# Layer 1's mixer weights split once, kept in DRAM scratch, and fetched in two parts

## The chip, the cores and the metric

The kernel runs on one core of a Trainium2 chip. The metric is device time in microseconds (us) for one execution; three runs of the kernel before took 1915.36, 1915.76 and 1921.28 us, median 1915.76. TensorE is called PE, VectorE DVE, ScalarE ACT, GpSimd POOL; SP issues most of the DMAs, POOL the others. PE's clock stands at one of two levels, 1.2 or 2.4 GHz; the profile gives it as a share of the higher one.

## The reference, cut to what matters

Two layers; the latent stream has 512 tokens, the context stream 256, both 1024 wide. Both use the same weights. In layer 1 the context serves only for its keys and values.

```python
for i in range(DEPTH):                       # DEPTH = 2
    last = i == DEPTH - 1
    # adaln: six modulation vectors of 1024 from ada_w[i] (1024 x 6144)
    h_l = rmsnorm(x, norm1_g[i]) * (1.0 + sc1_l) + sh1_l
    h_c = rmsnorm(ctx, norm1_g[i]) * (1.0 + sc1_c) + sh1_c
    p_l = h_l @ w_in[i]                      # hyena | gated MLP | attention
    p_c = h_c @ w_in[i]
    # queries of x attend to the keys of ctx and of x in one softmax
    x = x + g1_l * mix_out(p_l, att_l, hy_params, sg_params, w_out[i])
    x = x + g2_l * swiglu(rmsnorm(x, norm2_g[i]) * (1.0 + sc2_l) + sh2_l, ffn_w1[i], ffn_w2[i])
    if not last:
        ...                                  # the same for ctx
```

Inside `mix_out`, hyena convolves with filters computed by a small network from the weights alone (`hyena_filters`), through a Fourier transform that the kernel does with tables.

## The kernel before, in words

**Products in three parts.** Each float32 operand is split into a high part (rounded by an ACT copy) and a low part (a DVE subtraction), in `split` (L230 to L233). `mm3` (L251 to L253) then makes three matmuls, each on 128x128 blocks.

**Weights.** `weights` (L235) loads a weight tile of at most 128x1024 (512 KB) through SP into the arena FW and splits it into two blocks of the arena RW. RW holds 24 units of 256 floats per partition, that is three split tiles; FW holds six raw ones. `Columns` makes two such tiles out of `w_out` or the feed-forward weights, `win` two out of a chunk of `w_in`, `proj_cm` uses one. In layer 1 the context and the latent stream each load and split the chunks 7 to 10 of `w_in` for themselves.

**Arenas.** R (104 units) holds activations and tables. A task that will need room there first reserves it with `claim` and gives it back with `unclaim`; while the sum of reservations would pass 104, `claim` yields "wait" and the task goes no further. F (44 units) holds float32 data.

**Order.** The program is written by tasks in `network`: `lat_task`, `con_task`, `side_task` (the hyena filters' spectra, `spectra`), `ada_task` (the modulation vectors). `woven` takes the next step of the task that has least cost for its rate; a step that says "wait" costs a little and writes nothing. So a task that cannot get its reservation stands still while others go on writing. A scheduler then fixes one order for each engine, which the engine follows without overtaking; each instruction waits for semaphores of what it reads or overwrites.

**The end of layer 0's mixer.** `second` of `lat_mixer` ends the projections; the word "late" is set, and `spectra` of layer 1 may then start: it reserves 18*2+4 = 40 units. The latent stream meanwhile runs `outproj` over six of eight groups (24 units) and the second attention (`attend`, 12 units, with the latent queries, keys and values' 24 and the context keys and values' 8), and reserves 32 units for the input of its feed-forward part. The context's own feed-forward input holds 16. `ada_task` writes layer 1's six sections at the same time: 48 loads of 512 KB into FW, each pair followed by eight small matmuls (L400), with no wait but FW. Layer 0's feed-forward part (`ffn`, both streams) follows, then layer 1.

Of the kernel before, what the change touches and what calls it, by code (L numbers as in the profile page):

```python
# [16 lines left out]
P = 128  # L17
# [21 lines left out]
class Buf:  # L39


    def __init__(self, arena, pos, units, ap):
        self.arena, self.pos, self.units, self.ap = arena, pos, units, ap
# [69 lines left out]
class Stream:  # L113


    def __init__(self, name, T, v, home, away, mine):
# [12 lines left out]
CON = [9.69, 5.75, 2, 0.75, 1.53, 5, 22.61]  # L129
SIDE = [2.59, 3, 8.68, 2.5, 5.1, 16.97, 0.64]  # L130
ADA = [3.0, 0.6, 1.74, 0.52, 8.5, 2, 2]
WOVEN = [[11.5, 12.75, 10.55, 5.68, 7.8, 6.8, 3.47, 5.43, 8.37, 16.82],
         [8.7, 11.57, 10, 5.22, 3.19, 2.44, 5.22, 7.5, 49.17, 6.8]]

# [15 lines left out]
class Net:  # L150
    def __init__(self, ctx, tc, A):
        self.tc, self.nc, self.A = tc, tc.nc, A
        self.n = 0
        self.cost = 0
        self.phase, self.rates = None, {}
        self.claimed = 0
        self.const = ctx.enter_context(tc.tile_pool(name="const", bufs=1))
        psum = ctx.enter_context(tc.tile_pool(name="psum", bufs=1, space=bass.MemoryType.PSUM))
        for name, n in UNITS.items():
            t = self.const.tile([P, n * 256], F32R if name[0] == "R" else F32, name=name, tag=name)  # L160
            setattr(self, name, Arena(t, n, 256, {"RW": 4, "FW": 4}.get(name, 1)))
        self.B = Arena(psum.tile([P, 8 * 512], F32, name="banks", tag="banks"), 8, 512)
        self.tiny = self.const.tile([P, 40, 16], F32, name="tiny", tag="tiny")
        self.inv = self.const.tile([P, 8, 4], F32, name="inv", tag="inv")
        self.turn = 0
# [66 lines left out]
        self.nc.scalar.activation(hi, src, AF.Copy)  # L232
        (lo_eng or self.nc.vector).tensor_tensor(lo, src, hi.bitcast(F32), op=ALU.subtract)  # L233

    def weights(self, src, *shape, pool=False, arena=None):  # L235

        arena = arena or self.RW
        w = Pair(arena.get([P, *shape]), arena.get([P, *shape]))
        raw = self.FW.get([P, *shape])
        self.nc.sync.dma_start(raw.ap, src)  # L240
        self.split(raw.ap, *w.ap, self.nc.gpsimd if pool else None)
        raw.free()
        return w
# [273 lines left out]

    def proj_cm(self, st, l, n, out):

        w = self.weights(self.A["w_in_cm"][l, n], KT, P, pool=n % 2 and self.pool(st, "in cm"))  # L520
        self.mm3(out, [(w[:, k], st.h[k].ap) for k in range(KT)])
        w.free()

# [8 lines left out]

    def win(self, st, l, c):

        return [self.weights(self.A["w_in_tm"][l, c - 4, :, 4 * i:4 * i + 4], 4, CW, pool=i and self.pool(st, "in tm")) for i in range(2)]


    def qk(self, st, l, c, i, rope):
# [448 lines left out]
    def fwd(self, data, tabs, kdram, o, L, groups):  # L987

        nc = self.nc
        n = L // 256
        U = []
        for cs in range(2):
            yield from self.room(n, n, n)
            pe, po = self.ps(groups, n, HYW), self.ps(groups, n, HYW)
            for f in range(n):
                self.dft(pe[:, f], tabs[0], cs, f, [data[0][:, m] for m in range(n)], n)
                self.dft(po[:, f], tabs[1], cs, f, [data[1][:, m] for m in range(n)], n)
            e = self.f(n, HYW)  # L1000
            nc.scalar.activation(e.ap, pe.ap, AF.Copy)
            pe.free()
            u = [self.f(n, HYW) for _ in range(2)]
            nc.vector.tensor_tensor(u[0].ap, po.ap, e.ap, op=ALU.add)
            if cs == 0:
                nc.vector.tensor_tensor(u[1].ap, e.ap, po.ap, op=ALU.subtract)
            else:
                nc.vector.tensor_tensor(u[1].ap, po.ap, e.ap, op=ALU.subtract)
            po.free()
            e.free()  # L1010
            U.append(u)
            if cs == 0:
                yield
        for s in (*data, tabs[0]):
            s.free()
        yield from self.room(2 * n, n, n, n)
        Y = []
        for i in range(2):
            kd = self.f(2, n, HYW)
            nc.sync.dma_start(kd.ap, kdram[:, o, i])  # L1020
            kr, ks = kd[:, 0], kd[:, 1]
            ur, us = U[0][i].ap, U[1][i].ap
            t, y = self.f(n, HYW), self.f(n, HYW)
            e1, e2 = (nc.gpsimd if POOL[z][L == CTX] else nc.vector for z in ("product 1", "product 2"))
            e1.tensor_tensor(t.ap, us, ks, op=ALU.mult)
            nc.vector.tensor_tensor(y.ap, ur, kr, op=ALU.mult)  # L1026
            e2.tensor_tensor(us, us, kr, op=ALU.mult)
            nc.vector.tensor_tensor(ur, ur, ks, op=ALU.mult)  # L1028
            nc.vector.tensor_tensor(y.ap, y.ap, t.ap, op=ALU.subtract)
            nc.vector.tensor_tensor(ur, ur, us, op=ALU.add)  # L1030
            for b in (t, kd, U[1][i]):
                b.free()
            Y.append((y, U[0][i]))
        out, fs = [], []
        for c, op in ((0, ALU.add), (1, ALU.subtract), (0, ALU.subtract), (1, ALU.add)):
            fs.append(self.f(n, HYW))
            nc.vector.tensor_tensor(fs[-1].ap, Y[0][c].ap, Y[1][c].ap, op=op)
            out.append(Pair.one(self.r(2, n, HYW)))
            nc.scalar.activation(out[-1].hi, fs[-1].ap, AF.Copy)  # L1039
        for f, s in zip(fs, out):  # L1040
            nc.vector.tensor_tensor(s.lo, f.ap, s.hi.bitcast(F32), op=ALU.subtract)  # L1041
            f.free()
        for y in Y:
            for b in y:
                b.free()
        return out
# [84 lines left out]
    def outproj(self, st, l, ks, last=False):  # L1131

        T = st.T
        yield from self.claim(T // 128 * len(ks))
        mix = self.pairs(len(ks), T)
        for i, k in enumerate(ks):
            self.split(st.mix[k].ap, *mix[i].ap, self.nc.gpsimd if i % 2 < self.pool(st, "mix") else None)
            st.mix[k].free()
        yield
        yield from self.room(T // 256, T // 256, T // 128)  # L1140
        if last:
            st.acc = self.f(T)
        for c in range(4):
            yield from self.room(T // 256, T // 128)
            w = Columns(self, self.A["w_out"][l, 2 * c:2 * c + 2, :, ks[0]:ks[-1] + 1], len(ks), pool=self.pool(st, "out"))
            xb = self.x_open(st, c)
            for m in range(2):
                p = self.ps(st.mine, T)
                self.mm3(p.ap, [(w(m, i), mix[i].ap) for i in range(len(ks))])
                self.residual(st, l, 2, 2 * c + m, p.ap, xb[:, m])  # L1150
                p.free()
                if last:
                    self.square(st, 2 * c + m, xb[:, m])
                w.done(m)
            self.x_close(st, c, xb, st.away)
            yield
        st.home = st.away
        for b in mix:
            b.free()
        self.unclaim(T // 128 * len(ks))  # L1160

    def outproj_last(self, st, l, ks, parts):
# [1 line left out]
        nk, n = len(ks), st.T // parts  # L1164
        st.acc = self.f(st.T)
        src = self.A["w_out"][l, :, :, ks[0]:ks[-1] + 1].rearrange("m p k n -> p m k n")
        w = [self.weights(src[:, 4 * i:4 * i + 4], 4, nk, P) for i in range(2)]
        for i in range(parts):
            c = slice(i * n, (i + 1) * n)
            mix = self.pairs(nk, n)  # L1170
# [110 lines left out]
class Pair:  # L1281
# [6 lines left out]
    def one(buf):  # L1288
        return Pair(buf[:, 0], buf[:, 1], buf)

    @property
    def ap(self):
        return (self.hi, self.lo) if self.whole else (self.hi.ap, self.lo.ap)
# [9 lines left out]
class Columns:  # L1303
# [1 line left out]

    def __init__(self, net, src, k, pool=False, arena=None, hold=False):
        self.hold = hold
        if k <= 4:  # L1310
            self.w = [net.weights(src.rearrange("m p k n -> p m k n"), 2, k, P, pool=pool, arena=arena)]
        else:
            self.w = [net.weights(src[m], k, P, pool=pool and m, arena=arena) for m in range(2)]

    def __call__(self, m, k):
        return self.w[0][:, m, k] if len(self.w) == 1 else self.w[m][:, k]
# [30 lines left out]
def network(ctx, tc, A):  # L1347
# [15 lines left out]
    half = [slice(0, SEQ // 2), slice(SEQ // 2, SEQ)]  # L1363

    def phase(i):
        net.enter(i, lat=10, con=CON[i], side=SIDE[i], ada=ADA[i])

    def wait(*keys):
        while not done.issuperset(keys):
# [105 lines left out]
    def side_task():  # L1475
# [3 lines left out]
        yield from wait("late")  # L1479
        yield from spectra(1, SEQ)  # L1480

    def ada_task():
        yield from net.ada(0, (0, 1), "S", net.first)
        yield from mark((0, "mod0"))
        yield from net.ada(0, (2, 3, 4))
        yield from mark((0, "mod1"))
        yield from net.ada(0, (5,))
        yield from mark((0, "mod2"))
        yield from net.ada(1, (0, 1))
        yield from mark((1, "mod0"))  # L1490
        yield from net.ada(1, (2, 3, 4, 5))
        yield from mark((1, "mod1"), (1, "mod2"))
# [17 lines left out]
    for g, n in START:  # L1510
        run(take(gens[g], n))
    run(woven((lat_gen, "lat"), (con_gen, "con"), (side, "side"),
              (ada, "ada")))


def flat(ap):
# [106 lines left out]
```

## Time and profile before

| | us |
|---|---|
| median of 3 runs | 1915.76 |
| profiled execution | 1918.05 |
| its span, first to last instruction | 1916.3 |
| PE busy in the span | 1797.2 |
| DVE busy | 1079.3 |
| ACT busy | 676.9 |
| DMA: 245.39 MB, mean | 128 GB/s |

Layer 0's mixer ends at about 648 us, its feed-forward part at about 1190 us, layer 1's mixer at about 1560 us. A busy time is the union of the instructions' spans on an engine. The profile writes each of the small float32 matmuls of L400 as two records.

### The profile page before, as it was taken

Reading aid. Unit: us, or ns where it says so; the run is one execution under the profiler, and the core shown is the slowest. Engines: PE = TensorE matmul, PEld = TensorE weight load, DVE = VectorE, ACT = ScalarE, POOL = GpSimd, SP = SyncE. Lnnn points to the kernel's source line nnn. Section 1 sums busy time; section 2 is a strip of 40 time slices with the busy share of each in tenths; the row PEclk is TensorE's granted clock in tenths of the full one; section 3 lists DMA queues with packets and bytes.
Section 4 is the critical chain, followed back from the end, with each engine's and each line's share of the span. In section 5 each row is a group of like instructions: output and inputs, shape, how many; then the busy total and the mean of one; then the engine's idle time right before and its main releaser. Section 6 shows DMA issues by size and latency. Waiting matters only on the chain.

```text
span 1916.3 us, 27513 instructions
## 1 busy us (share of the span) xinstructions
PE 1797.2 (94%) x10938; PEld 1532.3 (80%) x10938; DVE 1079.3 (56%) x2243; ACT 676.9 (35%) x1167; POOL 118.0 (6%) x127
## 2 busy tenths in 40 slices
PE   4799898888997999999999999899999999999999
PEld 1478798677776888888888888789988798888887
DVE  5677786876868533332323244779588773333333
ACT  2534434443535321212121222633455452222221
POOL 1100223311001000000000000011000000000000
PEclk9799899799997999999999999899999899999999
DMA  8667644335454434343424135453213222323321
GB/s 274 198 222 237 212 155 133 111 101 162 144 174 137 153 99 136 90 136 110 149 86 146 61 112 174 138 171 124 72 43 111 73 62 64 115 83 102 93 93 65
DMA packets 101819, 245.39 MB, mean 128 GB/s; under 512 B 9748, under 2 KB 21750, under 8 KB 101690
## 3 DMA queue, kind: packets, MB, share of 16 engines
q1 hardware_dynamic: 93450, 221.71, 36.3%
q0 software_dynamic: 8240, 21.92, 3.9%
q8 instruction: 86, 1.41, 0.3%
q14 instruction: 43, 0.35, 0.1%
HBM read 221.18 MB, written 22.41 MB: 127 GB/s over the span
## 4 chain that ended last, share of the span: by engine, by line
PE 72%; DVE 7%; ACT 2%; issue 1%; DMA 1%; POOL 0%; DVEq 0%; ACTq 0%
PE banks L251 23%; PE banks L252 22%; PE banks L253 22%; PE banks L706 1%; PE banks L400 1%; DVE tiny L686 1%; PE banks L279 1%; DMA F<-x_ctx 1%; DVE F L459 1%; DVE RW L233 0%; ACT F L506 0%; ACT F L691 0%; DVE F L1028 0%; DVE F L1189 0%; DVE F L1026 0%
## 5 line engine op out<-in xcount | busy, mean ns | idle before, releaser
L251 PE MATMUL banks<-R,RW 128*128 128x512 f32 (+1 forms) x1984 | 698.3, 353 | 8.1 <-ACT R L507 2.9
L252 PE MATMUL banks<-R,RW 128*128 128x512 f32 (+1 forms) x1984 | 695.2, 351 | 2.6 <-DVE R L510 2.6
L253 PE MATMUL banks<-R,RW 128*128 128x512 f32 (+1 forms) x1984 | 693.4, 350 | 1.7 <-DVE RW L233 1.7
L232 ACT ACTIVATE RW<-FW 128x1024 fp32r<-128x1024 f32 (+2 forms) x240 | 240.3, 1002 | 563.9 <-PE banks L252 427.5
L251 PEld LDWEIGHTS banks<-R,RW 128*128 128x128 f32 x1984 | 379.0, 191 | 66.8 <-issue 5.6
L252 PEld LDWEIGHTS banks<-R,RW 128*128 128x128 f32 x1984 | 378.8, 191 | 51.9 <-DVE R L510 3.9
L253 PEld LDWEIGHTS banks<-R,RW 128*128 128x128 f32 x1984 | 378.1, 191 | 50.1 <-DVE RW L233 2.1
L233 DVE TENSOR_TENSOR RW<-FW,RW 128x1024 fp32r<-128x1024 f32 (+2 forms) x228 | 263.1, 1154 | 243.5 <-ACT RW L232 225.7
L1189 DVE SCALAR_TENSOR_TENSOR F<-banks,mods,F 128x512 f32<-128x512 f32 (+1 forms) x192 | 116.3, 615 | 177.1 <-PE banks L253 150.6
L251 PE MATMUL banks<-R 128*128 128x256 f32 (+3 forms) x584 | 185.0, 336 | 30.7 <-ACT R L1039 12.3
L252 PE MATMUL banks<-RW,R 128*128 128x256 f32 x624 | 178.9, 287 | 2.3 <-DVE RW L233 2.2
L251 PE MATMUL banks<-RW,R 128*128 128x256 f32 x624 | 180.1, 289 | 0.8 <-ACT RW L232 0.7
L253 PE MATMUL banks<-RW,R 128*128 128x256 f32 x624 | 179.0, 287 | 0.0
L252 PE MATMUL banks<-R 128*128 128x256 f32 (+3 forms) x584 | 176.6, 316 | 0.0
L253 PE MATMUL banks<-R 128*128 128x256 f32 (+3 forms) x584 | 175.2, 312 | 1.3 <-DVE R L1041 1.3
L251 PEld LDWEIGHTS banks<-R 128*128 128x128 f32 (+1 forms) x584 | 114.8, 205 | 55.9 <-ACT R L1039 14.6
L1207 DVE TENSOR_TENSOR F<-F,banks 128x256 f32<-128x256 f32 (+1 forms) x71 | 40.0, 565 | 203.8 <-PE banks L253 189.9
L232 ACT ACTIVATE R<-F 128x512 fp32r<-128x512 f32 (+1 forms) x133 | 71.8, 550 | 222.9 <-DVE F L1207 159.8
L252 PEld LDWEIGHTS banks<-R 128*128 128x128 f32 (+1 forms) x584 | 117.5, 205 | 8.8 <-issue 3.0
L252 PEld LDWEIGHTS banks<-RW,R 128*128 128x128 f32 x624 | 120.8, 194 | 4.6 <-DVE RW L233 3.7
L251 PEld LDWEIGHTS banks<-RW,R 128*128 128x128 f32 x624 | 120.8, 194 | 3.7 <-issue 1.0
L253 PEld LDWEIGHTS banks<-RW,R 128*128 128x128 f32 x624 | 120.9, 194 | 0.7 <-issue 0.2
(158 smaller groups left out, 1681.1 us busy)
## 6 DMA issues: line engine op xcount, KB each, us to landing
FW<-in_ffn_w SPq DMA_DIRECT2D x104, 512.0 KB, 3.7
FW<-in_ada_w SPq DMA_DIRECT2D x96, 512.0 KB, 5.3
FW<-in_w_in_tm SPq DMA_DIRECT2D x50, 512.0 KB, 4.7
R<-in_tab POOLq DMA_DIRECT2D x28, 512.0 KB, 5.9
FW<-in_w_in_cm SPq DMA_DIRECT2D x24, 512.0 KB, 4.7
F<-x_ctx SPq DMA_DIRECT2D x36, 256.0 KB, 3.4
FW<-in_ffn_w SPq DMA_DIRECT2D x24, 384.0 KB, 3.1
x_ctx<-F SPq DMA_DIRECT2D x32, 256.0 KB, 2.4
```

Source lines behind the costliest of these rows:

```text
L232: self.nc.scalar.activation(hi, src, AF.Copy)
L233: (lo_eng or self.nc.vector).tensor_tensor(lo, src, hi.bitcast(F32), op=ALU.subtract)
L251: mm(out, lhsT=lh, rhs=rh, start=(i == 0), stop=False)
L252: mm(out, lhsT=lh, rhs=rl, start=False, stop=False)
L253: mm(out, lhsT=ll, rhs=rh, start=False, stop=(i == n - 1))
L279: nc.tensor.matmul(p1[:, t:t + 1], lhsT=sq[:, t * P:(t + 1) * P], rhs=self.ones[:, 0:1], start=True, stop=True)
L400: nc.tensor.matmul(pa[32 * j:32 * j + 32, :], lhsT=self.cv[:, k, :], rhs=ws[j // 2][:, j % 2, z], start=(k == 0), stop=(k == KT - 1), tile ...
L459: nc.vector.tensor_tensor(st.acc[:, cols], st.acc[:, cols], q.ap, op=ALU.add)
L686: nc.vector.tensor_reduce(m, b.ap, axis=AX.X, op=ALU.max)
L706: nc.tensor.transpose(p[:, i, z, :], ws[z][:, (a + i) * P:(a + i + 1) * P], self.ident)
L1189: self.nc.vector.scalar_tensor_tensor(x, p, self.mods[l][:, sec * 8 + k, st.v:st.v + 1], x, op0=ALU.mult, op1=ALU.add)
L1207: nc.vector.tensor_tensor(s.ap, s.ap, u, op=ALU.mult)
```

## The change

A fifth task, `pre_task`, waits for "late" and for layer 0's last modulation section, then runs `split_ahead` for layer 1. It reserves 16 units of R for its whole run. For each of 32 weight tiles (8 of the narrow `w_in`, 14 of the chunked one, 8 of `w_out` with 384 KB, 2 of `w_out`'s last two groups) it loads the tile through SP into F, splits it into a block of R, and stores high and low part together (1 MB, or 768 KB) from POOL's queue into a DRAM scratch tensor. `weights` then looks the tile up by key: where it is in scratch, one DMA on POOL's queue brings both parts into RW, and there is no raw load and no split. This holds for the context's use as well, so 40 raw loads and splits of layer 1 become 32 splits, 32 stores and 40 fetches. Two products of hyena's spectrum in layer 1 go from POOL to DVE.

```diff
+PRE = 0.75
@@ class Net
+    def split_ahead(self, l, mem):
+        yield from self.claim(16)
+        for key, src, shape in self.sources(l):
+            n = math.prod(shape)
+            yield from self.room(4)
+            raw, w = self.f(*shape), Pair.one(self.r(2, n))
+            self.nc.sync.dma_start(raw.ap, src)
+            self.split(flat(raw.ap), *w.ap)
+            raw.free()
+            self.presplit[key] = mem(f"split{len(self.presplit)}", [P, 2, n])
+            self.nc.gpsimd.dma_start(self.presplit[key], w.whole.ap)
+            w.free()
+            self.cost += 1.0
+            yield
+        self.unclaim(16)
+
-    def weights(self, src, *shape, pool=False, arena=None):
+    def weights(self, src, *shape, pool=False, arena=None, key=None):
         arena = arena or self.RW
+        if key in self.presplit:
+            n = math.prod(shape)
+            w = Pair.one(arena.get([P, 2, n]))
+            self.nc.gpsimd.dma_start(w.whole.ap, self.presplit[key])
+            return w.shaped(shape)
...
-            e1, e2 = (nc.gpsimd if POOL[z][L == CTX] else nc.vector for z in ("product 1", "product 2"))
+            e1, e2 = (nc.gpsimd if POOL[z][L == CTX] and not self.presplit else nc.vector for z in ("product 1", "product 2"))
...
     def phase(i):
-        net.enter(i, lat=10, con=CON[i], side=SIDE[i], ada=ADA[i])
+        net.enter(i, lat=10, con=CON[i], side=SIDE[i], ada=ADA[i], pre=PRE)
...
+    def pre_task():
+        yield from wait("late", (0, "mod2"))
+        yield from net.split_ahead(1, lambda name, shape: tc.dram_tile(shape, F32R, name=name))
...
     run(woven((lat_gen, "lat"), (con_gen, "con"), (side, "side"),
-              (ada, "ada")))
+              (ada, "ada"), (pre_task(), "pre")))
```

`sources` lists the 32 tiles in the order 8 narrow and 14 chunked tiles of `w_in`, then `w_out`; `proj_cm`, `win`, `outproj` (through `Columns`) and `outproj_last` pass the keys.

In the new order the line numbers move: L441 is L400 of before, L418 is L377, L947 and L948 are the filter matmuls L905 and L906, L405 is the modulation load L364, L281 the raw load L240, L927 the filters' loads L885, L929 and L932 their splits L887 and L890, L234 the split L232, L292 to L294 `mm3`. L261 is the new raw load, L265 its store.

PE's order before, where the latent output projection over six groups ends (the R,RW rows; L400 is the modulation, the R rows are the second attention):

```order
L251 MATMUL banks<-R,RW 128x512
L252 MATMUL banks<-R,RW 128x512
L253 MATMUL banks<-R,RW 128x512
L400 MATMUL banks<-FW,cv_82 32x256 x8
L251 MATMUL banks<-R 128x512
L252 MATMUL banks<-R 128x512
```

PE's order after, at the same place:

```order
L294 MATMUL banks<-R,RW 128x512
L441 MATMUL banks<-FW,cv_82 32x256 x16
L418 MATMUL banks<-ident_100,F 128x128 x2
L441 MATMUL banks<-FW,cv_82 32x256 x24
L418 MATMUL banks<-ident_100,F 128x128 x2
L441 MATMUL banks<-FW,cv_82 32x256 x32
...
L418 MATMUL banks<-ident_100,F 128x128 x2
L947 MATMUL banks<-R 128x512
L948 MATMUL banks<-R 128x512
```

The left-out rows are three more runs of 32. All that is left of layer 1's modulation, 168 matmuls, now stands in one run with the spectra's first matmul (L947) behind it, and the attention has moved behind the spectra.

SP's order before, at that place (modulation, feed-forward weights, then the filters' loads L885):

```order
L364 DMA FW<-in_ada_w 128x2x512 x8
L240 DMA FW<-in_ffn_w 128x1024 x2
L364 DMA FW<-in_ada_w 128x2x512 x4
L240 DMA FW<-in_ffn_w 128x1024
L885 DMA F<-in_hy_w 64x1024 x2
L885 DMA F<-hid 64x512 x2
```

SP's order after (it issues in this order, and a load whose block isn't free holds up those behind it):

```order
L261 DMA F<-in_w_in_tm 128x1024 x4
L405 DMA FW<-in_ada_w 128x2x512 x12
L261 DMA F<-in_w_in_tm 128x1024
L405 DMA FW<-in_ada_w 128x2x512 x14
...
L261 DMA F<-in_w_out 128x768 x7
L281 DMA FW<-in_w_out 128x4x256
L261 DMA F<-in_w_out 128x768
...
L261 DMA F<-in_w_out 128x4x256
L281 DMA FW<-in_ffn_w 128x1024
L927 DMA F<-hid 64x512 x2
```

From the row of 12 on there are 36 loads L405 and 22 raw loads L261 up to L927; the filters' loads now stand behind the last raw load.

ACT's order before, at the splits L890 and L887 of the filters, which the first filter matmul reads:

```order
L507 ACTIVATE R<-F 128x256 x2
L691 ACTIVATE F,tiny<-banks,tiny,rq_81 128x768
L890 ACTIVATE R<-F 128x1024
L232 ACTIVATE R<-banks 128x512
L887 ACTIVATE R<-F 128x512
```

ACT's order after, at the same splits (L932 and L929):

```order
L449 ACTIVATE F<-banks 128x256
L234 ACTIVATE R<-F 128x1024 x8
L234 ACTIVATE R<-F 128x768 x3
L234 ACTIVATE RW<-FW 128x1024
...
L929 ACTIVATE R<-F 128x512
L234 ACTIVATE R<-F 128x768 x2
L234 ACTIVATE R<-F 128x1024
L932 ACTIVATE R<-F 128x1024
L234 ACTIVATE R<-F 128x1024
```

Of the 32 splits of the new task (R<-F of 1024 and 768) all but the last stand ahead of L932.

## Rows read from the trace of the kernel before

**Rows 1.** The page: busy time of each engine.
```profile
PE 1797.2 (94%) x10938; PEld 1532.3 (80%) x10938; DVE 1079.3 (56%) x2243; ACT 676.9 (35%) x1167; POOL 118.0 (6%) x127
```
**Rows 2.** Windows by stage: bounds, length, busy (instructions), granted clock, DMA share, GB/s.
```profile
490.00:556.00 66.00, 65.44 (x400) 51.27 (x402) 45.51 (x107) 30.23 (x60) 0.00 (x0) 1.00 0.40 129
556.00:648.00 92.00, 80.01 (x572) 63.97 (x563) 72.06 (x186) 46.11 (x98) 10.37 (x12) 0.89 0.48 150
648.00:1190.00 542.00, 541.75 (x3250) 471.69 (x3250) 182.79 (x259) 114.51 (x168) 3.21 (x6) 1.00 0.38 118
1190.00:1240.00 50.00, 42.14 (x199) 35.31 (x198) 37.92 (x91) 27.06 (x45) 0.53 (x1) 0.86 0.50 153
1240.00:1560.00 320.00, 306.37 (x2052) 275.63 (x2051) 252.79 (x579) 153.07 (x276) 17.80 (x18) 0.95 0.31 98
```
**Rows 3.** The page: chain that ended last, by engine.
```profile
PE 72%; DVE 7%; ACT 2%; issue 1%; DMA 1%; POOL 0%; DVEq 0%; ACTq 0%
```
**Rows 4.** PE's waits, 1200 to 1560 us, the longest two.
```profile
PE banks L251 <- ACT R L507: 6.3, 2, 3.4
PE banks L251 <- ACT R L1039: 4.9, 3, 4.1
```
**Rows 5.** DVE's groups by shape, 1200 to 1560 us.
```profile
L233 DVE TENSOR_TENSOR RW<-FW,RW 128x1024 fp32r<-128x1024 f32 x33 | 40.3, 1220 | 30.6 <-ACT RW L232 30.4
L1028 DVE TENSOR_TENSOR F<-F 128x512 f32<-128x512 f32 x4 | 6.6, 1657 | 0.1
L1026 DVE TENSOR_TENSOR F<-F 128x512 f32<-128x512 f32 x4 | 5.9, 1481 | 0.1
L584 DVE TENSOR_TENSOR F<-F 128x512 f32<-128x512 f32 x8 | 5.5, 684 | 0.1
```
**Rows 6.** SP's timeline where the changed order first differs.
```profile
489.22 0.33 SPq L443 DMA_DIRECT2D x_ctx<-F  x1
491.07 0.38 SPq L364 DMA_DIRECT2D FW<-in_ada_w  x1
```
**Rows 7.** PE's timeline at the latent output projection's end.
```profile
555.64 1.07 PE L400 MATMUL banks<-FW,cv 128*32 128x256 f32 x16
...
559.87 0.28 PE L252 MATMUL banks<-R,RW 128*128 128x256 f32 x1
559.99 0.29 PE L253 MATMUL banks<-R,RW 128*128 128x256 f32 x1
```
**Rows 8.** Modulation matmuls from 556 us on: ns min/median/max, first and last start.
```profile
L400 PE MATMUL banks<-FW,cv x336: 379/379/404, 555.6 to 1020.0; 128*32 128x256 f32 x168
```
**Rows 9.** DMA issues: KB each, median us from issue to landing.
```profile
FW<-in_ada_w SPq DMA_DIRECT2D x96, 512.0 KB, 5.3
FW<-in_w_in_tm SPq DMA_DIRECT2D x50, 512.0 KB, 4.7
R<-in_tab POOLq DMA_DIRECT2D x28, 512.0 KB, 5.9
kv<-R SPq DMA_DIRECT2D x4, 512.0 KB, 5.5
```
**Rows 10.** Windows of 10 us with the busiest DMA, and one after a wait.
```profile
10.00:20.00 10.00, 0.88 (x3) 0.16 (x1) 5.01 (x8) 3.04 (x5) 0.00 (x0) 1.00 1.03 371
30.00:40.00 10.00, 4.54 (x42) 1.68 (x36) 10.00 (x20) 1.60 (x3) 0.00 (x0) 0.83 0.92 294
40.00:50.00 10.00, 5.08 (x44) 1.99 (x40) 6.72 (x27) 3.74 (x7) 0.00 (x0) 1.00 0.88 297
110.00:120.00 10.00, 9.72 (x66) 7.40 (x64) 6.47 (x11) 4.99 (x7) 0.00 (x0) 1.00 0.85 274
1180.00:1190.00 10.00, 10.00 (x58) 8.76 (x57) 7.17 (x14) 4.17 (x8) 0.09 (x1) 1.00 0.86 278
1210.00:1220.00 10.00, 5.70 (x15) 4.38 (x16) 8.10 (x28) 6.57 (x11) 0.00 (x0) 0.50 0.29 80
```
**Rows 11.** The page: ACT's half of a weight split.
```profile
L232 ACT ACTIVATE RW<-FW 128x1024 fp32r<-128x1024 f32 (+2 forms) x240 | 240.3, 1002 | 563.9 <-PE banks L252 427.5
```

More of the change, by code (lines that the diff above doesn't have):

```diff
@@ L156, in __init__ @@
         self.claimed = 0
+        self.presplit = {}
         self.const = ctx.enter_context(tc.tile_pool(name="const", bufs=1))
@@ L233, in split, with sources, cm, tm @@
         (lo_eng or self.nc.vector).tensor_tensor(lo, src, hi.bitcast(F32), op=ALU.subtract)
-    def weights(self, src, *shape, pool=False, arena=None):
-        arena = arena or self.RW
+    def sources(self, l):
+        A = self.A
+        def cm(*ns):
+            return [(("in", l, n, 0), A["w_in_cm"][l, n], (KT, P)) for n in ns]
+        def tm(*cs):
+            return [(("in", l, c, 1 + i), A["w_in_tm"][l, c - 4, :, 4 * i:4 * i + 4], (4, CW)) for c in cs for i in range(2)]
+        yield from cm(4, 5, 0, 1, 2, 3)
+        yield from tm(7, 9, 8, 10, 5)
+        yield from cm(6, 7)
+        yield from tm(4, 6)
+        for m in range(KT):
+            yield ("out", l, m), A["w_out"][l, m, :, 0:6], (6, P)
+        rows = A["w_out"][l, :, :, 6:8].rearrange("m p k n -> p m k n")
+        for i in range(2):
+            yield ("last", l, i), rows[:, 4 * i:4 * i + 4], (4, 2, P)
+    def split_ahead(self, l, mem):
[14 more added lines that the diff above has]
+    def weights(self, src, *shape, pool=False, arena=None, key=None):
+        arena = arena or self.RW
+        if key in self.presplit:
[3 more added lines that the diff above has]
+            return w.shaped(shape)
         w = Pair(arena.get([P, *shape]), arena.get([P, *shape]))
@@ L518, in proj_cm @@
     def proj_cm(self, st, l, n, out):
-        w = self.weights(self.A["w_in_cm"][l, n], KT, P, pool=n % 2 and self.pool(st, "in cm"))
+        w = self.weights(self.A["w_in_cm"][l, n], KT, P, pool=n % 2 and self.pool(st, "in cm"), key=("in", l, n, 0))
         self.mm3(out, [(w[:, k], st.h[k].ap) for k in range(KT)])
@@ L533, in win @@
     def win(self, st, l, c):
-        return [self.weights(self.A["w_in_tm"][l, c - 4, :, 4 * i:4 * i + 4], 4, CW, pool=i and self.pool(st, "in tm")) for i in range(2)]
+        return [self.weights(self.A["w_in_tm"][l, c - 4, :, 4 * i:4 * i + 4], 4, CW, pool=i and self.pool(st, "in tm"),
+                             key=("in", l, c, 1 + i)) for i in range(2)]
     def qk(self, st, l, c, i, rope):
@@ L1144, in outproj @@
             yield from self.room(T // 256, T // 128)
-            w = Columns(self, self.A["w_out"][l, 2 * c:2 * c + 2, :, ks[0]:ks[-1] + 1], len(ks), pool=self.pool(st, "out"))
+            w = Columns(self, self.A["w_out"][l, 2 * c:2 * c + 2, :, ks[0]:ks[-1] + 1], len(ks), pool=self.pool(st, "out"),
+                        keys=[("out", l, 2 * c + m) for m in range(2)])
             xb = self.x_open(st, c)
@@ L1166, in outproj_last @@
         src = self.A["w_out"][l, :, :, ks[0]:ks[-1] + 1].rearrange("m p k n -> p m k n")
-        w = [self.weights(src[:, 4 * i:4 * i + 4], 4, nk, P) for i in range(2)]
+        w = [self.weights(src[:, 4 * i:4 * i + 4], 4, nk, P, key=("last", l, i)) for i in range(2)]
         for i in range(parts):
@@ L1289, in one, with shaped @@
         return Pair(buf[:, 0], buf[:, 1], buf)
+    def shaped(self, shape):
+        names = "abcdef"[:len(shape)]
+        cut = lambda t: t.rearrange(f"p ({' '.join(names)}) -> p {' '.join(names)}", **dict(zip(names, shape)))
+        return Pair(cut(self.hi), cut(self.lo), self.whole)
     @property
@@ L1303, with __init__ @@
 class Columns:
-    def __init__(self, net, src, k, pool=False, arena=None, hold=False):
+    def __init__(self, net, src, k, pool=False, arena=None, hold=False, keys=(None, None)):
         self.hold = hold
@@ L1312, in __init__ @@
         else:
-            self.w = [net.weights(src[m], k, P, pool=pool and m, arena=arena) for m in range(2)]
+            self.w = [net.weights(src[m], k, P, pool=pool and m, arena=arena, key=keys[m]) for m in range(2)]
     def __call__(self, m, k):
```

## Prediction

> **What bounds the kernel now.** I read the busy times first, then the windows by stage, the chain, PE's waits in layer 1's mixer, the DMA issues, and last the order of the changed kernel. PE is busy for 1797.2 of 1916.3 us [rows 1] and has 72% of the chain that ended last, DVE 7%, ACT 2%, DMA 1% [rows 3]. By stage: in layer 0's feed-forward part PE is busy for 541.75 of 542 us; ACT (114.51) and DVE (182.79) have room there, and the DMA engines move 118 GB/s at a share of 0.38 [rows 2]. In layer 1's mixer PE idles for 50 - 42.14 = 7.9 us in its first 50 us and for 320 - 306.37 = 13.6 us in the rest [rows 2]. The longest of these waits are for ACT L507 (the norm's output, 6.3 us) and ACT L1039 (hyena's spectrum, 4.9 us) [rows 4]; a wait for a split weight is not among them. So the work that the change takes out of layer 1 is already beside PE, and its time is worth little there. What it adds must find a place where neither PE nor what PE waits for is held up.
>
> **What layer 1 gains.** 40 splits go, each 1.00 us on ACT [rows 11] and up to 1.22 us on DVE [rows 5]: 40 us and 45 us of engine time. It could end at most the 4.9 us for L1039 and a part of the norm's 6.3; the bound is 13.6 us, nothing is the other. I take 4. The two products moved from POOL to DVE add 8 instructions of about 0.68 us (L584, the same shape without POOL beside it), 5.5 us. DVE's own four L1026 and four L1028 take 1.48 and 1.66 us while POOL multiplies, 12.5 us together [rows 5]; at 0.68 they would be 5.5, so DVE does 16 for 11 us. I cost this edit at nothing. The Trainium skill, "SBUF — State Buffer", section "Who interferes with whom", says that a DVE instruction with two SBUF inputs and a POOL instruction that reads SBUF block each other; by it the 1.48 and 1.66 fall to 0.68, and had these rows kept their length, DVE's 16 products would take 25 us and the edit cost some 13.
>
> **What layer 1 pays.** A tile now comes as one 1 MB DMA on POOL's queue. The nearest row is 512 KB on that queue, 5.9 us [rows 9]; for 1 MB I bound it by 5.9 and 11.8. RW still holds three split tiles, but before, the next tile lay raw in FW and needed only 2.2 us of ACT and DVE once a block was free. Where two tiles belong to one chunk, the next chunk's second tile can be asked for when the first tile of the old chunk is read out, some 23 matmuls before it is needed; these follow each other by 0.12 us [rows 7], 2.8 us. Bare, each of the 11 chunk changes (4 context, 7 latent) would show 3.1 to 9 us; the order puts hyena's matmuls between most of them. I take 4 changes at 3, 12 us, and bounds of 0 and 40. Behind a fetch that waits for its block stand the next fetches, the tables and the keys' loads, all on POOL's queue; DVE and ACT don't wait for it. Layer 1 nets +8, from -13 to +40.
>
> **Where the new work lands.** The code speaks of the feed-forward part, but the order puts nearly all of it ahead of it. When "late" is set the reservations are 24 + 8 + 12 (second attention), 16 (context) and 24 (output projection), 84 of 104. The new task adds 16. When the projection returns its 24, 76 remain; the spectra want 40 and the latent stream 32, and 76 + 32 = 108 already passes 104. Without the 16 both would have fitted one after the other, 60 + 40 = 100. So spectra, attention's rest and feed-forward all say "wait" until the new task has written its 32 tiles, and the modulation, which reserves nothing, writes all it has. This is what the order shows: on PE a run of 168 modulation matmuls and then L947; on SP the filters' loads behind the last raw load; on ACT the filter's split L932 behind 31 of the 32 new splits. PE cannot pass L947, so it waits there for DMA.
>
> **How long that wait is.** PE's order up to there holds the same matmuls as before, which end at 555.6 us [rows 7]. The transfers that must be done from then on: 36 modulation loads of 0.524 MB, 18.9; 22 raw loads (14 of 0.524, 8 of 0.393), 10.5; stores: R gives the task six blocks in rotation, so the 31st split waits for the 25th store, which leaves 19 stores at this point (16 of 1.05 MB, 3 of 0.79), 19.1; output and feed-forward weights and filter loads, 5.0. Together 53.5 MB. Before it, from the first changed issue at about 490 us [rows 6], the engines have some 10 raw loads and 6 stores more, 11.5 MB on top of 66 us at 129 GB/s, 8.5 MB [rows 2]: 20 MB in 66 us, 303 GB/s, so nothing is done ahead. The rate of a full DMA stretch: the five busiest 10 us windows give 371, 294, 297, 274 and 278 [rows 10], mean 303 GB/s. 53.5 MB / 303 = 177 us; at 371 it is 144, at 274 it is 195. Splits (2.2 us) are shorter than their transfers (1.57 MB, 5.2 us) and hide. I take 177, the mean, since loads, splits and stores follow each other in a ring of six blocks. The Trainium skill, "DMA: Bandwidth & Descriptors", section "Specifications", sets an HBM limit of about 358 GB/s for a core; by that the wait could not be below 149 us. The 371 of [rows 10] lies above it, so I keep 144 as the end.
>
> **What the wait gives back.** The 168 modulation matmuls run inside it. The trace has 336 records from 555.6 us on [rows 8], 16 to a group of 1.07 us [rows 7]: 21 groups, 22.5 us. Of these 13.4 groups (14.4 us) lay in the feed-forward part where PE was full; the others lay where PE also idled (80.01 busy of 92) [rows 2]. I take 18, between 14 and 22.
>
> **After the wait.** The spectra start alone, without the attention beside them, and PE's clock is low after a wait: the window after the norm of layer 1 has 0.50, that is its lower level, for 10 us [rows 10], which costs 5 us at most. I take 9 in all, from 0 to 20.
>
> **Sum.** On the profiled 1918.05 us: +177 - 18 + 9 + 8 = +176. The profiled execution lies 2 us above the median, so the forecast is 1916 + 174 = 2090 us. Lows and highs of the terms together: 144 - 22 - 13 = +109, 2025 us; 195 - 14 + 20 + 40 = +241, 2157.
>
> **Rivals.** (1) The wait is short because the DMA engines run nearer their peak: from 490 us on 73 MB at 371 GB/s end at 687 us, 131 after PE arrives; with the best of the other terms, +131 - 22 - 13 = +96, about 2010. For it: the 371 row; against it: that row is a stretch of loads alone, this one is 40% stores. Chance 0.09. (2) The stores set the pace, not the bandwidth: one after the other on POOL's queue at twice the 5.9 us of its 512 KB loads, 19 x 11.8 = 224 us; +224 - 18 + 9 + 8 = +223, about 2140, with its own high at 2190. Against it: six blocks may be under way at once; and 512 KB kv stores land in 5.5 us [rows 9]. The same skill page on SBUF, section "SBUF: two separate sides", warns that a DVE copy in a two-port mode starves the writing of descriptors for POOL's DMAs; the splits here are subtractions with two inputs, so I add no time for it. Chance 0.12. (3) The other side: PE is not held, because what L947 reads comes in time. Then the gains are left: -13 - 14 = -27, about 1890. That decides as soon as the wait is under some 20 us, so 53.5 MB would have to move at 2700 GB/s, or the order would have to be other than the reservations make it. Chance 0.03. (4) No change: the wait just pays for the gains, 0.02.
>
> **Chances.** The forecast, bandwidth-bound wait, has 0.74 and lies from 2025 to 2155. With parts of rivals 1 and 2 the range 2025 to 2155 holds 8 in 10. A run of this kernel tells about 0.3% from no change, 6 us: faster 0.03, same 0.02, slower 0.95.
>
> **What would show it.** In the profile after: between about 556 and 735 us PE nearly idle but for L441, DMA at a share near 0.9 and some 300 GB/s, SP waiting in it; PE's first later matmul L947 released by ACT or DVE on a filter split. The feed-forward part about 14 us shorter, without L441. In layer 1's mixer PE's new waits on the fetches L277, DVE's products at 0.68 us. The forecast is wrong if the window at 556 to 735 shows PE full, if it ends before 690 or after 780, or if layer 1's mixer moves by more than 40 us.

## The result, and the profile after

The changed kernel takes 2079.28 us (median of four runs, 2073.03 to 2085.33), the kernel before 1915.79 us beside it: a ratio of 1.0846, 95% interval 1.0804 to 1.0888. The profiled execution took 2073.03 us, its span is 155.0 us longer than the one of before. The page's busy times and its chain by engine, which answer [rows 1] and [rows 3]:

```profile
PE 1834.2 (89%) x10938; PEld 1548.0 (75%) x10938; DVE 1073.8 (52%) x2243; ACT 671.3 (32%) x1159; POOL 143.9 (7%) x191
PE 58%; issue 15%; DVE 5%; DMA 3%; ACT 2%; POOL 1%; POOLq 0%; ACTq 0%; DVEq 0%; SPq 0%
```

PE has the same 10938 matmuls and is busy for 37 us longer, so some ran at a lower clock; it is idle for 237 us rather than 119. The windows by stage (bounds, length, busy, granted clock, DMA share, GB/s), beside [rows 2], show where:

```profile
490.00:559.00 69.00, 65.30 (x378) 51.67 (x378) 47.76 (x107) 33.48 (x62) 2.72 (x6) 0.95 0.60 210
559.00:711.00 152.00, 51.13 (x357) 16.21 (x355) 34.27 (x39) 29.90 (x36) 13.81 (x26) 0.60 1.04 390
711.00:810.00 99.00, 74.32 (x382) 59.51 (x382) 67.26 (x161) 38.50 (x83) 11.41 (x13) 0.76 0.32 116
810.00:1360.00 550.00, 548.29 (x3174) 486.25 (x3174) 198.41 (x296) 125.67 (x188) 5.34 (x10) 1.00 0.30 95
1360.00:1718.00 358.00, 335.83 (x2190) 301.32 (x2191) 239.76 (x624) 140.31 (x276) 24.82 (x47) 0.95 0.47 154
```

From 559 to 711 us the DMA engines are busy throughout (mean share 1.04) and PE has almost only the modulation's matmuls. PE's waits in that stretch and the next (engine, what it waited for, us in total, times, longest) name the end of it, and PE's timeline its moment:

```profile
PE banks L947 <- DVE R L933: 64.7, 1, 64.7
PE banks L441 <- DMA FW<-in_ada_w: 30.2, 29, 5.0
PE banks L292 <- DMA R<-in_tab: 8.9, 1, 8.9
PE banks L418 <- ACT F L449: 8.0, 6, 5.6
```

```profile
560.52 0.39 PE L294 MATMUL banks<-R,RW 128*128 128x512 f32 x1
560.84 0.42 PE L441 MATMUL banks<-FW,cv 128*32 128x256 f32 x4
...
713.14 0.79 PE L947 MATMUL banks<-R 128*128 128x512 f32 x1 [64.69 <-DVE R L933]
```

The output projection ends at 560.8 us (555.6 before, [rows 7]), and the spectra's first matmul starts at 713.1: 152.3 us. It waits for the filter's low part (L933) on DVE. To add up the whole I take three marks that every kernel has: layer 0's first SiLU, its last, and layer 1's first, read from ACT's timeline (a first one begins with the load of its table, L1249 after).

| us | first SiLU | feed-forward part, first to last SiLU | layer 1's mixer, to its first SiLU |
|---|---|---|---|
| before | 639.4 | 539.9 | 383.6 |
| after | 810.0 | 524.0 | 383.9 |
| after the spectra (e1) | 638.6 | 562.7 | 396.3 |
| no stores (e2) | 736.0 | 524.0 | 378.4 |
| no reservation (e3) | 651.1 | 592.6 | 383.9 |
| modulation later (e4) | 748.4 | 545.8 | 390.2 |
| products only (e5) | 637.4 | 540.8 | 377.7 |
| e1 at rate 0.65 (e6) | 635.9 | 554.3 | 383.1 |
| e1 without stores (e7) | 640.3 | 541.3 | 378.1 |
| e6, fetch on two queues (e8) | 640.0 | 555.5 | 392.2 |
| e6, block held (e9) | 634.5 | 549.6 | 387.6 |
| products on POOL (e10) | 813.9 | 523.9 | 387.2 |

Before, 83.8 us lie between the output projection's end and the first SiLU; after, 96.8 us between L947 and the first SiLU. So +5.2 up to the projection's end, +152.3 for the wait, +13.0 behind it, -15.9 in the feed-forward part, +0.3 in layer 1's mixer: +154.9 of the 155.0.

Each row of the table is one profiled execution, and executions of one kernel lie up to 21 us apart (e4: 2022.61 to 2043.40 us). A part of that is PE's clock, which differs between executions: in the mixer of before, e5, e2, after and e1, in this order, the same 2333 matmuls keep PE busy for 359 to 370 us (columns as above, PE's busy time and the clock first and sixth).

```profile
1179.30:1562.90 383.60, 362.11 (x2333) 323.17 (x2332) 301.40 (x688) 186.82 (x335) 18.92 (x21) 0.94 0.35 111
1178.20:1555.90 377.70, 359.03 (x2333) 320.24 (x2333) 298.19 (x696) 186.36 (x334) 6.42 (x13) 0.95 0.35 112
1259.90:1638.40 378.50, 359.72 (x2334) 321.00 (x2333) 298.13 (x696) 186.42 (x335) 6.43 (x13) 0.95 0.35 112
1333.90:1717.80 383.90, 360.73 (x2333) 323.02 (x2333) 258.25 (x656) 149.93 (x294) 27.56 (x53) 0.95 0.49 162
1201.30:1597.60 396.30, 370.39 (x2333) 330.59 (x2332) 258.23 (x656) 149.90 (x294) 27.50 (x53) 0.92 0.47 157
```

PE's idle time in the mixer, its length less the busy time, is the steadier measure there: 21.5 us before, 23.2 after, 25.9 in e1, 18.8 in e2 and 18.7 in e5.

### The profile page after: what moved, and what is told of

Its sections match the earlier page's. It is cut to its first block, busy times and chain, and to the rows that moved or that the text cites. A ratio compares the mean times of both kernels' runs of the same rounds, so it can differ in the third digit from the quotient of the medians.

```text
span 2071.3 us, 27596 instructions
## 1 busy us (share of the span) xinstructions
PE 1834.2 (89%) x10938; PEld 1548.0 (75%) x10938; DVE 1073.8 (52%) x2243; ACT 671.3 (32%) x1159; POOL 143.9 (7%) x191
## 4 chain that ended last, share of the span: by engine, by line
PE 58%; issue 15%; DVE 5%; DMA 3%; ACT 2%; POOL 1%; POOLq 0%; ACTq 0%; DVEq 0%; SPq 0%
PE banks L292 19%; PE banks L293 18%; PE banks L294 18%; PE banks L748 1%; DMA RW<-split 1%; POOL split L265 1%; DVE tiny L728 1%; DMA R<-in_tab 1%; DVE R L235 1%; DMA F<-x_ctx 1%; PE banks L320 0%; ACT F L733 0%; ACT R L234 0%; DVE F L500 0%; DVE RW L235 0%
## 5 line engine op out<-in xcount | busy, mean ns | idle before, releaser
L292 PE MATMUL banks<-R,RW 128*128 128x512 f32 (+1 forms) x1984 | 698.0, 353 | 12.4 <-ACT R L548 5.1
L294 PE MATMUL banks<-R,RW 128*128 128x512 f32 (+1 forms) x1984 | 695.3, 351 | 1.7 <-DVE RW L235 1.7
L292 PEld LDWEIGHTS banks<-R,RW 128*128 128x128 f32 x1984 | 379.9, 192 | 68.1 <-ACT R L548 6.5
L294 PEld LDWEIGHTS banks<-R,RW 128*128 128x128 f32 x1984 | 380.3, 192 | 50.1 <-DVE RW L235 2.1
L234 ACT ACTIVATE RW<-FW 128x1024 fp32r<-128x1024 f32 (+2 forms) x200 | 199.7, 999 | 507.8 <-PE banks L293 390.4
L235 DVE TENSOR_TENSOR RW<-FW,RW 128x1024 fp32r<-128x1024 f32 (+2 forms) x188 | 217.0, 1155 | 223.5 <-ACT RW L234 221.9
L292 PE MATMUL banks<-R 128*128 128x256 f32 (+3 forms) x584 | 186.1, 338 | 44.5 <-ACT F L733 11.8
L234 ACT ACTIVATE R<-F 128x512 fp32r<-128x512 f32 (+3 forms) x165 | 103.6, 637 | 297.9 <-DVE F L1250 167.5
L292 PE MATMUL banks<-RW,R 128*128 128x256 f32 x624 | 181.9, 292 | 5.2 <-DMA RW<-split 4.9
L294 PE MATMUL banks<-RW,R 128*128 128x256 f32 x624 | 179.8, 288 | 0.0
L293 PE MATMUL banks<-R 128*128 128x256 f32 (+3 forms) x584 | 178.6, 318 | 0.2 <-DVE R L235 0.2
L294 PE MATMUL banks<-R 128*128 128x256 f32 (+3 forms) x584 | 178.0, 315 | 0.4 <-DMA R<-in_tab 0.2
L292 PEld LDWEIGHTS banks<-R 128*128 128x128 f32 (+1 forms) x584 | 115.4, 207 | 69.6 <-issue 16.0
L235 DVE TENSOR_TENSOR R<-F,R 128x512 fp32r<-128x512 f32 (+3 forms) x157 | 111.4, 715 | 91.3 <-ACT R L234 89.6
L441 PE MATMUL banks<-FW,cv 128*32 128x256 f32 x768 | 91.2, 476 | 52.7 <-DMA FW<-in_ada_w 52.6
L292 PEld LDWEIGHTS banks<-RW,R 128*128 128x128 f32 x624 | 121.7, 195 | 8.9 <-DMA RW<-split 5.7
L293 PEld LDWEIGHTS banks<-RW,R 128*128 128x128 f32 x624 | 122.1, 196 | 5.7 <-DVE RW L235 4.4
```

The source lines that it names most:

```text
L292: mm(out, lhsT=lh, rhs=rh, start=(i == 0), stop=False)
L293: mm(out, lhsT=lh, rhs=rl, start=False, stop=False)
L294: mm(out, lhsT=ll, rhs=rh, start=False, stop=(i == n - 1))
L441: nc.tensor.matmul(pa[32 * j:32 * j + 32, :], lhsT=self.cv[:, k, :], rhs=ws[j // 2][:, j % 2, z], start=(k == 0), stop=(k == KT - 1), tile ...
```

## Experiments

Theory A: the reservation orders the stream behind the 32 tiles, and PE waits for bytes over bandwidth. Theory B: the traffic and the splits cost wherever they stand. Later theories stand with their runs. Ratios are to the kernel before on the same chip; its median was 1920.26 us beside e1 to e4, 1915.74 beside e5 to e8 and 1917.89 beside e9 and e10, so across these groups the ratios compare better than the times.

**The task begins after the spectra (e1).**

```diff
-        yield from wait("late", (0, "mod2"))
+        yield from wait("late", (0, "mod2"), (1, SEQ))
```

> One edit to the changed kernel: the new task also waits until layer 1's spectra are done in program order, so that its reservation of 16 falls into the feed-forward part (32 + 16 + 24 + 16 = 88 of 104). All loads, splits, stores and fetches stay. Theory A (the reservation makes the stream wait for 32 tiles, and that alone costs): the wait of PE at 559 us is gone, 1905 to 1925 us. Rival B (the extra traffic and split work cost wherever they stand: 47 MB on top of 118 GB/s in the feed-forward part, 32 splits on ACT and DVE): PE idles inside the feed-forward part, which grows, 1940 to 2000 us.

1949.71 us, ratio 1.0158 (1.0119 to 1.0197). The wait is gone: the first SiLU stands where it stood before (638.6). But theory A's "that alone" falls, since the feed-forward part is 22.8 us longer, with PE idle for 18.8 us in it rather than 1.3, and the mixer 12.7, of which 8.3 are PE's busy time at the lower clock of this execution and 4.4 its idle time. What ACT waited for between 636 and 1190 us has a row that neither the kernel before nor e7 can have, since they have no stores:

```profile
ACT R L234 <- DMA split<-R: 57.4, 10, 9.8
```

A split's ACT copy waits for a store that still reads the block, and behind it on ACT's queue stand the feed-forward part's own splits. PE's longest waits there are for an ACT copy of this line, L234, and for a DVE instruction:

```profile
PE banks L292 <- ACT R L234: 12.8, 2, 7.1
PE banks L292 <- DVE F L979: 4.4, 1, 4.4
```

**No reservation, same start (e3).** The splits go to RW, so the blocks change along with the reservation.

```diff
-        yield from self.claim(16)
...
-            raw, w = self.f(*shape), Pair.one(self.r(2, n))
+            raw, w = self.f(*shape), Pair.one(self.RW.get([P, 2, n]))
...
-        self.unclaim(16)
```

> The changed kernel without the reservation of 16: the new task begins at the same point, but splits into blocks of the weights' arena RW, for which nothing is reserved. Theory A (the reservation orders the stream behind the tiles): spectra and latent stream go on beside the tiles, 1905 to 1930 us. Rival E (the place is wrong even without a reservation, since raw loads stand on SP's queue ahead of filter loads and the stores hold blocks that the stream's own weights want): PE still waits before the spectra, 1950 to 2080 us.

1984.84 us, 1.0350 (1.0302 to 1.0397): E's range, but not E's place. The first SiLU is only 11.7 us late, against 170.5 in the changed kernel, so without the reservation nearly all of the wait goes. The other 52.7 us came in the feed-forward part, where the three blocks of RW are shared with the weights and PE idles for 34.8 us. That the sharing causes it fits ACT's waits for the stores, but no run shows it apart from the other costs of the stores. Who waited for the stores in this run, most of all:

```profile
ACT RW L234: 116.0, 19
```

**No stores (e2).**

```diff
-            self.presplit[key] = mem(f"split{len(self.presplit)}", [P, 2, n])
-            self.nc.gpsimd.dma_start(self.presplit[key], w.whole.ap)
+            self.presplit["any"] = None
```

> The changed kernel without the 32 stores: tiles are still loaded, split and released, but layer 1 loads and splits its mixer weights itself, as before (the two products stay on DVE). Theory A (the wait is bytes over DMA bandwidth): some 19 MB of the wait's 53 MB go, 49 us at 390 GB/s, so 2030 us (2015 to 2045). Rival C (the wait is paced by something other than bytes, as the loads standing in line on SP or the splits): no change, 2070 to 2090 us. Rival D (the stores set the pace one by one on POOL's queue): the wait falls by far more than 49 us, below 2000 us.

1995.28 us, 1.0400 (1.0361 to 1.0438): 84 us under the changed kernel (85 by the ratios), more than A's 49, and 5 us inside the range that I gave to D. L947's counterpart starts at 643.9, 69.2 us earlier. The windows:

```profile
490.00:559.00 69.00, 65.55 (x421) 49.30 (x421) 50.68 (x98) 37.06 (x66) 0.00 (x0) 0.99 0.59 200
559.00:644.00 85.00, 36.44 (x291) 11.94 (x284) 27.85 (x31) 25.14 (x29) 2.16 (x4) 0.70 1.04 362
```

From 490 us to the end of the wait 69 x 200 + 85 x 362 = 13.8 + 30.8 = 44.6 MB moved; in the changed kernel 69 x 210 + 152 x 390 = 14.5 + 59.3 = 73.8 MB. The difference of 29 MB at 390 GB/s is 75 us. So A's mechanism holds and my 49 was too small: it left out the six stores issued before 559 us, whose bytes also put off what is behind them, and 28 stores rather than 25 had landed when the wait ended. The DMA share is 1.04 with the stores and 1.04 without them; had they come one by one with the engines waiting, as in D, it should be lower with them.

**The modulation after the spectra (e4).**

```diff
+        yield from wait((1, SEQ))
         yield from net.ada(1, (0, 1))
```

> The changed kernel with one edit: layer 1's modulation waits until layer 1's spectra are done in program order, so that its 36 loads (18.9 MB) and 168 matmuls leave the wait and go back beside the feed-forward part. Theory A (bytes over bandwidth): the wait falls by 18.9 MB / 390 GB/s = 48 us, the feed-forward part gets its 16 us back, 2079 - 48 + 16 = 2047 us (2030 to 2060). Rival C (the ring of load, split and store paces the wait, the modulation's loads only fill gaps): the wait stays and the feed-forward part grows, 2085 to 2100 us.

2039.03 us, 1.0609 (1.0552 to 1.0667), 40 us under the changed kernel (45 by the ratios); A's range. The spectra start 64.7 us earlier, with 69 x 247 + 90 x 374 = 50.7 MB moved, and the feed-forward part is 21.8 us longer:

```profile
490.00:559.00 69.00, 65.90 (x362) 52.96 (x360) 55.42 (x116) 39.79 (x71) 4.30 (x8) 0.98 0.70 247
559.00:649.00 90.00, 0.55 (x1) 0.29 (x1) 27.40 (x26) 23.39 (x25) 11.67 (x22) 0.51 1.00 374
```

With 73.8, 50.7 and 44.6 MB from 490 us on, the spectra's first matmul stands at 713, 648 and 644 us. The modulation did not only fill gaps (C). The bytes don't give each microsecond: e4 and e2 differ by 6 MB and only 4 us, since half of the 6 had moved before 559 us and the rates behind it were 374 and 362 GB/s.

**The products alone (e5).** On the kernel before (of the line that picks the two engines, the choice alone):

```diff
-nc.gpsimd if POOL[z][L == CTX] else nc.vector
+nc.gpsimd if POOL[z][L == CTX] and self.phase < 4 else nc.vector
```

> The kernel before with one part of the change: hyena's two products of layer 1 on DVE rather than POOL; nothing is split ahead. Theory H (DVE's own two products fall from 1.48 and 1.66 us to about 0.68 and the critical waits on ACT's spectrum get shorter, as the run without stores suggests, whose layer 1 mixer took 378.4 us against 383.6): 5 us faster than before, ratio 0.997. Rival I (the prediction's: the edit is worth nothing): ratio 1.000; the 5 us then come from somewhere else.

1912.98 us (12 runs) against 1915.74, 0.9979 (0.9966 to 0.9993): H's 0.997 lies in the interval, I's 1.000 doesn't. The medians lie 2.8 us apart (1.3 to 6.5 by the interval), and it is the one kernel of this study that is faster than both. Layer 1's mixer is 5.9 us shorter in the profiled executions, 2.8 of them PE's idle time (21.5 to 18.7) and 3.1 its busy time at a higher clock; whether the edit or the execution made the clock higher isn't shown. DVE's groups, which answer [rows 5]:

```profile
L1026 DVE TENSOR_TENSOR F<-F 128x512 f32<-128x512 f32 x4 | 2.7, 682 | 0.0
...
L1028 DVE TENSOR_TENSOR F<-F 128x512 f32<-128x512 f32 x4 | 2.7, 682 | 0.0
```

The 1481 and 1657 ns fell to 682, and PE's wait for the spectrum's split (L1039) from 4.9 us [rows 4] to 3.3:

```profile
PE banks L251 <- ACT R L1039: 3.3, 2, 2.5
```

**A lower rate (e6), and no stores (e7), both with e1's start.**

```diff
-PRE = 0.75
+PRE = 0.65
```

> Like the run that waits for the spectra, with the new task's rate at 0.65 rather than 0.75, so that the tiles spread more evenly over the feed-forward part. Theory J (its 23 us come from two or three tiles in direct succession, where ACT's split waits in line for a store to free a block and holds up the feed-forward part's own splits): fewer such places, 1925 to 1940 us. Rival B (the traffic costs wherever it stands): 1945 to 1955 us.

> Like the run that waits for the spectra, without the 32 stores; layer 1 loads and splits its mixer weights itself (the two products stay on DVE). Theory J (the split that waits for a store's block is what costs in the feed-forward part): that part falls back from 563 to 540 to 545 us, the whole to 1908 to 1920 us. Rival B (loads on SP's queue and splits cost by themselves): the part stays above 555 us, the whole above 1925 us.

e6: 1936.11 us, 1.0095 (1.0068 to 1.0122), in J's range. The feed-forward part is 8.4 us shorter than e1's, with 32.1 us of ACT's waits for stores, not 57.4. e7, which has e2's edit with e1's start: 1918.03 us, 1.0010 (0.9994 to 1.0025); the part is back at 541.3 us. So it is the stores that make the part longer: with loads and splits alone it is as long as before (539.9) and in e5 (540.8). The whole of e7 is still 5 us above e5, which shares its products, so loads and splits were not free. The first 80 us of the part, e6 and then e7:

```profile
640.00:720.00 80.00, 70.22 (x410) 59.87 (x410) 35.90 (x51) 26.95 (x41) 7.07 (x11) 0.94 0.76 261
```

```profile
640.00:720.00 80.00, 79.14 (x487) 68.93 (x488) 47.26 (x64) 34.89 (x50) 2.91 (x3) 1.00 0.65 217
```

**The block held longer (e9), to test J.**

```diff
+        last = None
...
-            w.free()
+            if last:
+                last.free()
+            last = w
...
+        last.free()
```

> Like the run with the rate 0.65, but the block of a stored tile is given back only when the next tile is written, so that the next split finds another one. Theory J (what is left of the cost in the feed-forward part is ACT waiting in line for a store that still reads its block: 57 us in ten waits at the rate 0.75, 32 in eight at 0.65, none without stores): these waits go, the feed-forward part falls from 554 to 541 to 547 us, the whole to 1919 to 1928 us. Rival M (the waits are only where the wire's time shows: 47 MB beside the weights' loads): the part stays at 552 to 557 us, the whole at 1930 to 1940.

1929.84 us, 1.0076 (1.0047 to 1.0105), which can't be told from e6's 1.0095 (1.0068 to 1.0122). The part is 549.6 us, between J's range and M's, and ACT still waits for stores:

```profile
ACT R L234 <- DMA split<-R: 40.6, 9, 8.5
```

So J as I put it falls: holding the block longer did not end ACT's waits. That the stores cost is shown (e7); whether by their blocks or by the wire they take from the raw loads stays open. In e9 PE waited for 0.4 us after 720 us, and 8.5 us before it, 6.5 of them in one wait for DVE.

**The fetch on two queues (e8).**

```diff
-            self.nc.gpsimd.dma_start(w.whole.ap, self.presplit[key])
+            self.nc.sync.dma_start(w.hi.bitcast(F32), self.presplit[key][:, 0].bitcast(F32))
+            self.nc.gpsimd.dma_start(w.lo, self.presplit[key][:, 1])
```

> Like the run with the rate 0.65, and each fetch of layer 1 cut in two: the upper parts by SP's queue, the lower parts by POOL's, 512 KB each. Theory K (PE's 6 to 9 us of waits on the fetches come from the length of one 1 MB transfer, 5 to 10 us): they halve, layer 1's mixer 4 to 6 us shorter than in the run with the rate 0.65. Rival L (the fetch waits for its block in RW, not for the wire): no difference between the two.

1945.64 us, 1.0153 (1.0126 to 1.0180): 10 us slower than e6, which neither K nor L foretold. K's premise fails in the trace: the halves took a median of 4.6 us to land (SP) and 5.4 (POOL), where e6's whole 1 MB took 5.2. PE's waits on fetches in layer 1's mixer are 7.3 us rather than 4.9. The other 7 us are PE's own: the same matmuls at a lower mean clock, here e6 and then e8; what lowered it stays open.

```profile
1190.00:1573.00 383.00, 361.12 (x2333) 323.51 (x2332) 258.06 (x656) 149.83 (x294) 27.79 (x53) 0.95 0.49 163
```

```profile
1196.00:1588.00 392.00, 367.84 (x2334) 327.50 (x2333) 258.16 (x656) 149.64 (x293) 27.22 (x52) 0.93 0.49 159
```

**The products back on POOL (e10), in the changed kernel** (again the choice alone).

```diff
-nc.gpsimd if POOL[z][L == CTX] and not self.presplit else nc.vector
+nc.gpsimd if POOL[z][L == CTX] else nc.vector
```

> The changed kernel with one edit undone: layer 1's two products stay on POOL as before. Theory H (products and fetches add: the products on DVE give 5 to 6 us, the fetches instead of splits take as much back): layer 1's mixer grows from 383.9 to about 389 us, the whole from 2079 to 2084 us. Rival N (beside the fetches, which are issued by POOL too, or without the splits on DVE, the edit is worth nothing): 383 to 385 us, 2079.

2081.56 us, 1.0863 (1.0816 to 1.0911). The mixer is 387.2 us, 3.3 more: between H and N, but 2.9 of the 3.3 are PE's busy time at a clock of 0.94 rather than 0.95, and PE's idle time is 23.6 us, 0.4 more. DVE's own products are slow again, 1.48 and 1.77 us, so the effect on DVE is there; what it is worth beside the fetches is undecided, since the totals (1.0846 and 1.0863) can't be told apart. e5 alone shows the edit's worth.

## Why the prediction was right

**The mechanism.** The order made from the reservations did what it said: PE idle but for L441, and L947 released by DVE's filter split. e3 and e1 show that the reservation at that place is the cause: with the same tiles from the same point, no reservation and other blocks (e3), 11.7 us are left of 170.5 at the first SiLU, and with the reservation and the blocks of R, but a later start (e1), none.

**How long the wait is.** Forecast 177 us, measured 152.3. The total of bytes from 490 us on was right, 73.5 MB forecast and 73.8 read from the windows. Two steps were off, and by luck in opposite directions. The step that failed is the rate: 303 GB/s was the mean of the five busiest windows of a kernel that never asks for more for long [rows 10]; in the wait, with requests in line throughout, it was 390. The second is "nothing is done ahead, 20 MB in 66 us": 14.5 MB moved in 69 us, so 59.3 and not 53.5 MB were left. At 390 GB/s the forecast's bytes would have given 137 us; the 5.8 MB more made it 152. So of the rate rival 1, with a chance of 0.09, was right: the engines ran above even its 371. Its 131 us failed since it let them run so from 490 us on, and the 69 us up to the wait saw 210 GB/s. I weighed the Trainium skill's limit of about 358 GB/s for a core ("DMA: Bandwidth & Descriptors", section "Specifications") and kept 371 as the end. The trace goes beyond both, 390 GB/s over 152 us; the measurement decides. Nothing else of the wait rests on that limit.

**Rival 2,** stores one after the other, falls: 32 stores were issued from 509.3 to 714.6 us, one per 6.6 us, while one took 9.6 us to land (median), so they overlapped:

```profile
L265 POOL DMA_DIRECT2D split<-R x32: 531/531/582, 509.3 to 714.6; - x32
DMA to landing us min/median/max: 6.8/9.6/15.9
```

**What the wait gives back.** Forecast -18, measured -15.9 in the feed-forward part; e4 moves the modulation out of the wait and the part grows by 21.8. Right; the few microseconds of the 18 that the forecast placed outside the feed-forward part count behind the wait here.

**Around the wait.** Behind it +9 was forecast and +13.0 measured, inside the range of 0 to 20; the 5.2 us ahead of it had no term: from 490 to 559 us PE idled for 3.7 us, against 0.6 in the 66 us before [rows 2], and its clock was 0.95 and not 1.00. The clock (0.76 from 711 to 810 us) was expected. The wait of 8.9 us for `in_tab` was not: the tables' loads stand on POOL's queue behind the last stores. The prediction named that only for the fetches.

**Layer 1.** Forecast +8 from -13 to +40, measured +0.3, and two terms that nearly cancel. The products, costed at nothing, took 2.8 us off PE's idle time in the mixer and off the medians (e5; the mixer 5.9 with the clock). The fetches instead of raw loads and splits cost 5.5 us (e2's mixer 378.4 to 383.9), 4.4 of them idle time, of a forecast +8. PE's waits on fetches in the mixer were 6.5 us, six of them, where four of 3 us were forecast. A fetch took 5.2 us to land (median, 4.4 to 10.1), mostly less than the lower bound of 5.9:

```profile
PE banks L292 <- DMA RW<-split: 6.5, 6, 2.6
```

What the 40 splits could give back was little, as read from [rows 4]: they were beside PE. From e2 to after DVE's busy time in the mixer falls by 40 us and ACT's by 36, near the 45 and 40 forecast, and PE's idle time doesn't fall with them; no run takes the splits away without fetches in their place. The Trainium skill's rule on two-input DVE instructions beside POOL ("SBUF — State Buffer", section "Who interferes with whom") agrees with e5's 682 ns in place of 1481 and 1657.

**Sum.** Terms 177 - 18 + 9 + 8 = 176 against 152.3 - 15.9 + 13.0 + 5.2 + 0.3 = 154.9 in the profiled executions. The medians lie 163.5 us apart, since the profiled execution of after was the shortest of its four, 6.2 us under their median, and that of before lay 2.3 above its own. The forecast's last sum takes the 2 us between profile and median off twice: 1916 + 176 is 2092, not 2090.

**What the change could have brought.** With the wait taken away the best versions that still fetch (e9 and e6) are 12 and 20 us above the kernel before, and e7, with loads and splits but no store or fetch, is level with it though it has the products' gain. So the forecast's sign did not hang on the reservation alone, as rival 3 (1890 without the wait) had it: against e7, stores lengthen the feed-forward part by 8 to 21 us (e9, e6, e1), and the fetches make the mixer longer, where less splitting was to make it shorter.

## What to carry to other kernels

Where tasks share a reserved space, add up the reservations at the point where a new one begins: a task that fits by itself can put another behind all of its work. Work that is beside the bottleneck is worth little when it is taken away, and a scratch copy adds its store and its fetch to queues on which others wait. For a stretch in which the DMA engines have requests in line throughout, the highest window (371 here) came nearer to the rate than a mean of busy ones (303 against 390); count all bytes queued ahead, also those from before the wait. Before a few microseconds of one profile are put down to an edit, see how much of them is PE's busy time at another clock.

## What the runs showed of the hardware

Loads and stores mixed moved at a mean of 390 GB/s for 152 us; the highest window of 20 us had 415, with PE at its lower clock:

```profile
660.00:680.00 20.00, 0.00 (x0) 0.00 (x0) 5.72 (x6) 4.64 (x5) 3.19 (x6) 0.50 1.06 415
```

The modulation's matmuls took a median of 631 ns in the wait and 379 before [rows 8]:

```profile
L441 PE MATMUL banks<-FW,cv x336: 379/631/637, 560.8 to 646.6; 128*32 128x256 f32 x168
```

With 51 us of PE's time in the wait at a mean clock of 0.60, they hid behind DMA all the same: PE then waited 64.7 us for L947. In e8 the halves of a fetch, at most 512 KB each, side by side on SP's and POOL's queues, landed after a median of 4.6 and 5.4 us, and e6's whole fetches, at most 1 MB, after 5.2.
